# First six projection units side by side, and a 64-row matmul inside both MLPs of a two-layer trunk

## The chip, the cores and the metric

The kernel runs on one core of a Trainium2 chip. The metric is the device time of one execution in microseconds (us). The kernel before has a median of 2397.32 us over 3 runs (2397.16 to 2398.94).

## The reference, cut to what matters

Two decoder layers run on one sequence of 256 tokens with model width 2048, all in float32:

```
for layer in range(2):
    h = rms_norm(x, norm_mix[layer])
    if layer == 0:
        u = h @ w_in_a                       # one projection for both head groups
        y = concat(nsa(u_nsa), rwkv7(u_rw)) @ w_out_a
    else:
        u = h @ w_in_b
        y = concat(rglru(u_lru), hgrn2(u_hg)) @ w_out_b
    x = x + y
    h2 = rms_norm(x, norm_mlp[layer])
    z = relu(h2 @ w_ff1[layer])              # 2048 -> 8192
    x = x + (z * z) @ w_ff2[layer]           # 8192 -> 2048
```

`rwkv7` mixes each token with the one before it, sends a part of its columns through small low-rank matrices (96, 96 and 256 wide) and runs a recurrence over 16 heads of 64. `nsa` is attention over compressed, selected and windowed keys. Nearly all of the arithmetic lies in the dense projections and in the MLPs.

## The kernel before, in words

Activations are kept transposed: 2048 features are 16 blocks ("k") of 128 partitions, with the 256 tokens along the free axis. A dense product is cut into **units** of 128 output columns. One unit reads 1 MB of weights in two halves; `load` (L123) issues one DMA per half on SyncE's queue into a pool of four buffers.

**Three products for one.** The array takes a rounded float32 format, so each operand is split into a high and a low part. `split` (L128) makes `wh` with a ScalarE copy (L130) and `wl` with a VectorE subtraction (L132), each into a pool of two buffers. An operand tile holds the activations' high part in its columns 0 to 255 and the low part in columns 256 to 511. `mm3` (L147) then runs for each k one pass of `wh` over 512 columns (L152) and one pass of `wl` over 256 columns (L153), both into one PSUM bank. Such a pass pair is called a pair here; a unit has 16 pairs. `evac` (L163) folds the bank into one 256-column tile with a ScalarE copy (L167) and a VectorE add (L168).

**The norm is late.** `prepare` (L192) scales x by the gain alone and splits it (L193 on ScalarE, L194 on VectorE). The mean square goes through a matmul with a matrix of ones (`rstd_of`, L206), and the factor 1/rms is multiplied in when a unit is evacuated (L306). So units can run before the norm is known.

**The start.** x comes in eight DMAs of 2 blocks (L255). The first unit's halves lie between them in the queue, then the second unit's, then the constants (L259). All sixteen blocks are prepared, with one split among each eight; unit 0 runs, the squares (L263 to L269) and unit 1's splits follow, then unit 1, the norm's matmul, units 2 and 3 and, in `rwkv_a` (L310), the rest. The first four units are the low-rank columns; from unit 4 on, three units (r, k, v) belong to each of eight steps j. Each j has low-rank matmuls of 96 rows (L350, L354), a chain of gates on ScalarE and VectorE, and a group under `behind()` (L378), which gets a lower priority and ends in 64-row matmuls (L425) and in DMAs to DRAM on GpSimd's queue. The recurrence's small systems are then solved on VectorE (`rw_solve`, L437) while TensorE goes on with the attention's units; `rwkv_b` (L450) needs the solution, fetched back at L466.

**The MLP.** `mlp` (L934) runs four blocks of 16 up-units and 16 down-units, 2048 pairs per layer, as one unbroken stream; the norm's matmul (L206) of the MLP lies among the first unit's pairs.

**The order.** The framework's planner orders each engine's instructions when the kernel is built, by priority (program order, moved by `high_priority` and `behind`) and by its own estimate of when operands are ready. Each engine then runs its own list strictly in that order. PSUM has eight banks: two with the tag "mm" for units and two each with "ga", "gb" and "gc". `keep_in_program_order` pins an instruction behind the one written before it on the same engine; `issue_after` queues what a block issues on an engine behind a given instruction, as an order alone.

Of the kernel before, what the change touches and what calls it, by code (L numbers as in the profile page):

```python
# [10 lines left out]
F32 = mybir.dt.float32  # L11
F32R = mybir.dt.float32r
# [7 lines left out]
P = 128  # L20
T = 256
D = 2048
KT = D // P
# [29 lines left out]
CON, NCON = _cols(_CON)  # L53
HG_LEVELS = (1, 2, 4, 8, 16, 32)
RWP_N = 4 * 512 + 4


@with_exitstack
def kernel(
# [52 lines left out]
    def bank(name, tag="ga"):  # L112
        return pg.tile([P, 512], F32, tag=tag, name=name)
# [6 lines left out]
        return [t[:, k] for t in (half_of(pool, f"{name}_{h}") for h in range(2)) for k in range(8)]  # L120


    def load(src, h, name, pool=None):  # L123
        raw = (pool or wraw).tile([P, 8, P], F32, tag="raw", name=f"raw_{name}_{h}")
        nc.sync.dma_start(raw, src[:, h * 1024 : (h + 1) * 1024].rearrange("p (b c) -> p b c", c=P))
        return raw

    def split(raw, h, name):  # L128
# [23 lines left out]
            M.matmul(ps, wh, mv, start=first, stop=False)  # L152
        M.matmul(ps[:, :T], wl, mv[:, :T], start=False, stop=last)  # L153

    def unit(src, mv, name, folded=False, tag=None, parts=None, pool=None):
        ps = bank(f"mm_{name}", tag) if tag else pmm.tile([P, 512], F32, tag="mm", name=f"mm_{name}")
        parts = parts or stream(src, name, pool)
        for k in range(KT):
            wh, wl = parts[k // 8]
            mm3(ps, wh[:, k % 8], wl[:, k % 8], mv[k], k == 0, k == KT - 1, folded)  # L160
        return ps

# [38 lines left out]
        A.activation(sq, x, AF.Square)  # L201
        V.tensor_add(acc, acc, sq)

    def rstd_of(acc, name):
        ps = bank(f"ms_{name}")
        M.matmul(ps[:, :T], ones, acc, start=True, stop=True)  # L206
        v = ev.tile([P, T], F32, tag="t", name=f"v_{name}")
        V.tensor_scalar(v, ps[:, :T], 1.0 / D, EPS, op0=ALU.mult, op1=ALU.add)
        r0 = ev.tile([P, T], F32, tag="s", name=f"r0_{name}")
        rsqrt_of(r0, v, 1.0, zero_b, name, ev)  # L210
        q = ev.tile([P, T], F32, tag="sq", name=f"q_{name}")
        V.tensor_mul(q, r0, r0)
        V.scalar_tensor_tensor(q, q, -0.5, v, ALU.mult, ALU.mult)
        r = ev.tile([P, T], F32, tag="rstd", name=f"rstd_{name}")
        V.scalar_tensor_tensor(r, q, 1.5, r0, ALU.add, ALU.mult)
        return r
# [15 lines left out]
    def layer0_mix():  # L232
        with ExitStack() as st:
            mx = st.enter_context(tc.tile_pool(name="mx", bufs=1))
            acc, hx = norm("a0")
            rwp_d = [dram.tile([P, 2, RWP_N], F32, name=f"rwp_d{j}") for j in range(4)]
            pm_d = [dram.tile([P, 2, 8, P], F32, name=f"pm_d{j}") for j in range(4)]
            z_d = dram.tile([P, 32, 32], F32, name="z_d")

            gate = mx.tile([P, T], F32, name="gate", bufs=1)  # L240
            nb = mx.tile([P, 32, 32], F32, name="nb", bufs=1)
            yr = half_of(big, "yr")
            cw = big.tile([P, 4, 8, P], F32, tag="half", name="cw")

            def load_cw(w):
                nc.sync.dma_start(cw.rearrange("p b l e -> p b (l e)"), cmp_w[w].rearrange("b p n -> p b n"))

            with tc.tile_pool(name="pa", bufs=1) as pa:
                xi = [pa.tile([P, 8, T], F32, tag="rwp", name=f"xi_{i}", bufs=2) for i in range(2)]
                raws = []  # L250
                first = []
                with tc.high_priority(10**6):
                    for i in range(2):
                        for b in range(4):
                            nc.sync.dma_start(xi[i][:, 2 * b : 2 * b + 2], xT[:, 8 * i + 2 * b : 8 * i + 2 * b + 2])  # L255
                        raws.append(load(w_in0[0], i, "i0_0"))
                    for i in range(2):
                        raws.append(load(w_in0[1], i, "i0_1"))
                    nc.sync.dma_start(con, consts)  # L259

                    def squares(i):
                        sq = pa.tile([P, 4, T], F32, tag="pm", name=f"sq_a0_{i}", bufs=2)
                        A.activation(sq, xi[i // 2][:, 4 * (i % 2) : 4 * (i % 2) + 4], AF.Square)  # L263
                        V.tensor_add(sq[:, 0:2], sq[:, 0:2], sq[:, 2:4])
                        if i == 0:
                            V.tensor_add(acc, sq[:, 0], sq[:, 1])
                        else:
                            V.tensor_add(sq[:, 0], sq[:, 0], sq[:, 1])
                            V.tensor_add(acc, acc, sq[:, 0])  # L269

                    parts = []
                    for i in range(2):
                        for j in range(8):
                            prepare(hx, 8 * i + j, xi[i][:, j], "gmix0")
                            if j == 3:
                                parts.append(split(raws[i], i, "i0_0"))
                    first.append(unit(None, hx, "i0_0", parts=parts))
                    squares(0)
                    parts = [split(raws[2], 0, "i0_1")]
                    squares(1)  # L280
                    parts.append(split(raws[3], 1, "i0_1"))
                    first.append(unit(None, hx, "i0_1", parts=parts))
                    squares(2)
                    squares(3)
                    rstd = rstd_of(acc, "a0")
                first.append(unit(w_in0[2], hx, "i0_2", tag="ga"))
                first.append(unit(w_in0[3], hx, "i0_3", tag="gb"))
                rwkv_a(pa, gate, hx, scaled_by(rstd), rwp_d, pm_d, nb, first, load_cw)
            with tc.tile_pool(name="pb", bufs=1) as pb, tc.tile_pool(name="pn", bufs=1) as pn:
                rw_solve(pb, nb, z_d)  # L290
                for j in range(0, 8, 2):
                    rwkv_b(pb, j, rwp_d, pm_d, z_d, yr)
                kv = nsa_keys(pn, mx, hx, scaled_by(rstd), gate, cw, load_cw)
                yn = half_of(big, "yn")
                for j in range(8):
                    nsa_head(pn, mx, hx, scaled_by(rstd), kv, j, yn)
        return [t[:, k] for t in (yn, yr) for k in range(8)]
# [9 lines left out]

        return scaled

    def rwkv_a(pa, gate, hx, scaled, rwp_d, pm_d, nb, first, load_cw):  # L310
        def tl(tag, shape=(P, T), bufs=1, name=None):
            return pa.tile(list(shape), F32, tag=tag, name=name or tag, bufs=bufs)

        def shifted(u, name, mu, out, rows=P):
            ub = tl("ub", (P, T + 1), 3, name=f"ub_{name}")
            G.memset(ub[:, 0:1], 0.0)
            scaled(first[u] if u < 4 else unit(w_in0[u], hx, f"i0_{u}"), ub[:, 1:], name)
            d = tl("d", bufs=2, name=f"d_{name}")
            V.tensor_sub(d[:rows], ub[:rows, 0:T], ub[:rows, 1:])
            V.scalar_tensor_tensor(out[:rows], d[:rows], p_("mu", mu)[:rows], ub[:rows, 1:], ALU.mult, ALU.add)  # L320
            return ub
# [15 lines left out]
        for j in range(8):  # L337
# [5 lines left out]
            pm = tl("pm", (P, 8, P), 2, name=f"pm_{j}")  # L343
            js = slice(j * P, (j + 1) * P)
            w2j = tl("w2j", (P, P), 2, name=f"w2_{j}")
            nc.scalar.dma_start(w2j[:96], rw_w2[:, js])
            a2j = tl("a2j", (P, P), 2, name=f"a2_{j}")
            nc.scalar.dma_start(a2j[:96], rw_a2[:, js])
            ps = bk_(f"lora_{j}")
            M.matmul(ps[:, :T], w2j[:96], th[:96], start=True, stop=True)  # L350
            sg = tl("sg", bufs=2, name=f"sg_{j}")
# [26 lines left out]
            with behind():  # L378
# [28 lines left out]
                nc.scalar.dma_start(g2j, rw_g2[:, :, j * P : (j + 1) * P])  # L407
# [526 lines left out]
    def mlp(layer, xs, hx, rstd, nxt, zp, zraw):  # L934
        z = {}

        def up(q):
            zq = z[q] = operand(big if q % 2 == 0 else zp, f"z_{layer}_{q}")
            for k in range(KT):
                n = f"f1_{layer}_{q}_{k}"  # L940
                s = evac(unit(w_ff1[layer, q * KT + k], hx, n, pool=zraw), n)
                V.tensor_mul(s, s, rstd)  # L942
                V.scalar_tensor_tensor(s, s, 0.0, s, ALU.max, ALU.mult)
                split_to(zq[k], s)

# [12 lines left out]
        down(1)  # L958
        up(3)
        down(2)  # L960
        down(3)
# [45 lines left out]
def _layout(i):  # L1007
# [17 lines left out]
    out["w_in0"] = _chunks(np.concatenate(cols, axis=1))  # L1025
# [108 lines left out]
```

## Time and profile before

| what | value |
|---|---|
| median of 3 runs | 2397.32 us |
| the profiled execution, its own time | 2415.31 us |
| its span, first to last instruction | 2413.5 us |
| TensorE busy | 2390.6 us (99%) |
| VectorE busy | 1697.7 us (70%) |
| ScalarE busy | 1243.7 us (52%) |
| mean granted TensorE clock | 0.997 |

The span is the time between the first and the last instruction of the profiled execution. Its own time is 1.8 us longer. Busy shares are means over stages with different limits. The end of a matmul in the trace is modelled and reaches into the next one, so the distance from start to start is what tells how fast a stream of passes runs.

### The profile page before, as it was taken

The numbers are of one execution on the slowest core, as the hardware profiler recorded it, in microseconds if no ns is written. First come the engines' busy times: TensorE is split into PE (matmuls) and PEld (weight loads), VectorE is DVE, ScalarE is ACT, GpSimd is POOL, SyncE is SP. The second block draws the span as 40 slices with busy tenths as digits, with TensorE's granted clock in tenths as the row PEclk, the third lists the DMA queues.
The fourth block names the chain that finished last, engine by engine and source line by source line (L and its number), as shares of the span: only waits on it lengthen the run. The fifth ranks groups of instructions, "written<-read, shape, count | busy, mean of one in ns | idle before, by whom it ended". The sixth has DMA issues, their size and how long they took to land.

```text
span 2413.5 us, 37947 instructions
## 1 busy us (share of the span) xinstructions
PE 2390.6 (99%) x14386; PEld 2072.1 (86%) x14386; DVE 1697.7 (70%) x3006; ACT 1243.7 (52%) x2152; POOL 44.9 (2%) x118
## 2 busy tenths in 40 slices
PE   8999999999999999999999999999999999999999
PEld 6888877798888888888888888889888888888888
DVE  7887865677676576576568888788777667667555
ACT  7554455555444444444456666675544444444443
POOL 0112010000000000000000000000000000000000
PEclk9999999999999999999999999999999999999999
DMA  7667743465555555655555444456556555656564
GB/s 263 212 216 228 246 139 105 155 209 183 190 184 186 188 184 187 188 185 187 187 176 187 150 151 153 154 168 217 185 191 191 189 188 191 192 187 190 191 199 134
DMA packets 125862, 446.77 MB, mean 185 GB/s; under 512 B 14192, under 2 KB 19952, under 8 KB 124016
## 3 DMA queue, kind: packets, MB, share of 16 engines
q1 hardware_dynamic: 115824, 414.06, 53.7%
q0 software_dynamic: 5456, 26.79, 3.1%
q10 hardware_dynamic: 4400, 3.50, 0.4%
q8 instruction: 114, 1.87, 0.3%
q14 instruction: 68, 0.56, 0.1%
HBM read 429.06 MB, written 15.22 MB: 184 GB/s over the span
## 4 chain that ended last, share of the span: by engine, by line
PE 93%; DVE 3%; DMA 2%; ACT 1%; issue 1%; POOL 0%; DVEq 0%; ACTq 0%; POOLq 0%
PE mm_f L152 39%; PE mm_f L153 20%; PE mm_i L152 13%; PE mm_i L153 7%; PE mm_o L153 2%; PE mm_o L152 1%; PE mm_o L149 1%; PE mm_o L150 1%; DVE wl_i L132 1%; PE hl L816 1%; PE pair L425 1%; DMA rwp<-rwp_d 1%; PE psx L496 0%; ACT wh_o L130 0%; PE psu L503 0%
## 5 line engine op out<-in xcount | busy, mean ns | idle before, releaser
L132 DVE TENSOR_TENSOR wl_f<-raw_f,wh_f 128x1024 fp32r<-128x1024 f32 x512 | 627.2, 1225 | 486.1 <-ACT wh_f L130 486.1
L130 ACT CAST wh_f<-raw_f 128x1024 fp32r<-128x1024 f32 x512 | 538.6, 1052 | 773.4 <-PE mm_f L152 566.8
L152 PE MATMUL mm_f<-hx_m,wh_f 128*128 128x512 f32 x2048 | 717.2, 395 | 0.0
L152 PE MATMUL mm_f<-z,wh_f 128*128 128x512 f32 x2048 | 717.1, 395 | 0.0
L152 PE MATMUL mm_i<-hx_a,wh_i 128*128 128x512 f32 x1536 | 563.9, 405 | 11.5 <-ACT wh_i L130 11.4
L153 PE MATMUL mm_f<-hx_m,wl_f 128*128 128x256 f32 x2048 | 574.8, 281 | 0.0
L153 PE MATMUL mm_f<-z,wl_f 128*128 128x256 f32 x2048 | 574.4, 280 | 0.0
L152 PEld LDWEIGHTS mm_f<-z,wh_f 128*128 128x128 f32 x2048 | 383.9, 187 | 90.0
L152 PEld LDWEIGHTS mm_f<-hx_m,wh_f 128*128 128x128 f32 x2048 | 383.9, 187 | 90.0
L153 PE MATMUL mm_i<-hx_a,wl_i 128*128 128x256 f32 x1536 | 447.6, 291 | 1.2 <-DVE wl_i L132 1.0
L153 PEld LDWEIGHTS mm_f<-hx_m,wl_f 128*128 128x128 f32 x2048 | 387.0, 189 | 0.1
L153 PEld LDWEIGHTS mm_f<-z,wl_f 128*128 128x128 f32 x2048 | 387.0, 189 | 0.0
L152 PEld LDWEIGHTS mm_i<-hx_a,wh_i 128*128 128x128 f32 x1536 | 289.8, 189 | 72.3 <-ACT wh_i L130 12.1
L153 PEld LDWEIGHTS mm_i<-hx_a,wl_i 128*128 128x128 f32 x1536 | 291.5, 190 | 9.3 <-DVE wl_i L132 4.0
L130 ACT CAST wh_i<-raw_i 128x1024 fp32r<-128x1024 f32 x192 | 201.3, 1049 | 188.9 <-PE mm_i L152 169.5
L132 DVE TENSOR_TENSOR wl_i<-raw_i,wh_i 128x1024 fp32r<-128x1024 f32 x192 | 234.5, 1222 | 80.6 <-ACT wh_i L130 76.4
L168 DVE TENSOR_TENSOR s_f<-mm_f,t_f 128x256 f32<-128x256 f32 x256 | 106.7, 417 | 3.0 <-ACT t_f L167 3.0
L132 DVE TENSOR_TENSOR wl_o<-raw_o,wh_o 128x1024 fp32r<-128x1024 f32 x64 | 78.3, 1223 | 32.6 <-ACT wh_o L130 32.3
L130 ACT CAST wh_o<-raw_o 128x1024 fp32r<-128x1024 f32 x64 | 67.2, 1050 | 63.3 <-issue 29.2
L167 ACT COPY t_f<-mm_f 128x256 f32<-128x256 f32 x256 | 93.2, 364 | 4.3 <-PE mm_f L153 4.3
L153 PE MATMUL mm_o<-ym,wl_o 128*128 128x256 f32 x256 | 72.6, 284 | 0.8 <-DVE wl_o L132 0.8
L942 DVE TENSOR_TENSOR s_f<-s_f,rstd_m 128x256 f32<-128x256 f32 x128 | 54.4, 425 | 4.4
(420 smaller groups left out, 2254.7 us busy)
## 6 DMA issues: line engine op xcount, KB each, us to landing
raw_f<-in_w_ff_dram SPq DMA_DIRECT2D x512, 512.0 KB, 4.5
raw_i<-in_w_in_dram SPq DMA_DIRECT2D x192, 512.0 KB, 4.1
raw_o<-in_w_out_dram SPq DMA_DIRECT2D x64, 512.0 KB, 4.2
rwp_d<-rwp POOLq DMA_DIRECT2D x8, 1026.0 KB, 7.1
rwp<-rwp_d POOLq DMA_DIRECT2D x4, 1540.0 KB, 10.7
cw<-in_cmp_w_dram SPq DMA_DIRECT2D x2, 2048.0 KB, 10.2
pm_d<-pm POOLq DMA_DIRECT2D x8, 512.0 KB, 6.3
pm<-pm_d POOLq DMA_DIRECT2D x4, 1024.0 KB, 5.3
```

The source lines that it names most:

```text
L130: A.copy(wh, raw)
L132: V.tensor_sub(wl, raw, wh)
L149: M.matmul(ps[:, :T], wh, mv[:, :T], start=first, stop=False)
L150: M.matmul(ps[:, :T], wh, mv[:, T:], start=False, stop=False)
L152: M.matmul(ps, wh, mv, start=first, stop=False)
L153: M.matmul(ps[:, :T], wl, mv[:, :T], start=False, stop=last)
L167: A.copy(t, ps[:, T:])
L168: V.tensor_add(s, ps[:, :T], t)
L425: M.matmul(pps[q][:, c * P : (c + 1) * P], bk[hs, c], ar[hs, c], start=True, stop=True)
L816: M.matmul(pl[:, x * T + i * P : x * T + (i + 1) * P], qk[:, ii], qk[:, ii], start=True, stop=True)
L942: V.tensor_mul(s, s, rstd)
```

## The change

**The first six units** run side by side. Their weights are laid out in DRAM so that block k of all six is one contiguous piece of 128 x 768 (a layout of the inputs, made before the launch). Sixteen DMAs bring them, one for each k, with the DMA of x's two blocks ahead of each even k and the constants behind k = 9. For each k the block is prepared, 768 columns are split at once, and six pairs go into six PSUM banks. Ahead of it, sixteen 128 x 128 matmuls of a zeroed tile are issued. The norm's matmul takes a bank of tag "gc", and a seventh unit follows it ahead of `rwkv_a`.

**DMAs.** The small low-rank weights on ScalarE's queue are issued behind the first copy of the start (`anchor`). The compression weights `cw` are issued behind the last weight load written before them.

**Both MLPs** get one matmul of 64 rows and 128 columns, between the `wh` and the `wl` pass of k = 4 in the second unit of the first block.

```diff
+NFIRST = 6
+    last_load = [None]
-        nc.sync.dma_start(raw, src[:, h * 1024 : ...])
+        last_load[0] = nc.sync.dma_start(raw, src[:, h * 1024 : ...])
+    def narrow(name):
+        ps = bank(f"nar_{name}")
+        tc.keep_in_program_order(M.matmul(ps[:, 0:P], ident[0:64], ident[0:64], start=True, stop=True))
     def unit(...):
+            if k == part_at:
+                M.matmul(ps, wh[:, k % 8], mv[k], start=False, stop=False)
+                narrow(name)
+                tc.keep_in_program_order(M.matmul(ps[:, :T], wl[:, k % 8], mv[k][:, :T], start=False, stop=False))
+                continue
     def load_cw(w):
+        with tc.issue_after(last_load[0].ins):
             nc.sync.dma_start(cw..., cmp_w[w]...)
+    wrm = pa.tile([P, P], F32, name="wrm")
+    V.memset(wrm, 0.0)
     with tc.high_priority(10**6):
-        for i in range(2):                       # x and the first unit's halves, then the second unit's
-            ...
-        nc.sync.dma_start(con, consts)
+        for k in range(KT):
+            if k % 2 == 0:
+                nc.sync.dma_start(xi[k // 8][:, k % 8 : k % 8 + 2], xT[:, k : k + 2])
+            nc.sync.dma_start(raw[:, :NFIRST], w_k[k].rearrange("p (b c) -> p b c", c=P))
+            if k == 9:
+                nc.sync.dma_start(con, consts)
+        for i in range(16):
+            M.matmul(pw[:, :P], wrm, wrm, start=True, stop=True)
-        ...                                      # sixteen prepares with two splits, unit 0, squares, unit 1
+        for k in range(KT):
+            prepare(hx, k, xi[k // 8][:, k % 8], "gmix0")
+            ins = A.copy(wh[:, :NFIRST], raws[k][:, :NFIRST])
+            anchor = anchor or ins.ins
+            V.tensor_sub(wl[:, :NFIRST], raws[k][:, :NFIRST], wh[:, :NFIRST])
+            for u in range(NFIRST):
+                mm3(first[u], wh[:, u], wl[:, u], hx[k], k == 0, k == KT - 1)
+            if k % 4 == 3:
+                squares(k // 4)
-        rstd = rstd_of(acc, "a0")
-    first.append(unit(w_in0[2], hx, "i0_2", tag="ga"))
-    first.append(unit(w_in0[3], hx, "i0_3", tag="gb"))
+        rstd = rstd_of(acc, "a0", "gc")
+    first.append(unit(w_in0[NFIRST], hx, f"i0_{NFIRST}", tag="gb"))
     ...
-        nc.scalar.dma_start(w2j[:96], rw_w2[:, js])
+        with tc.issue_after(anchor):             # the same for a2j and g2j
+            nc.scalar.dma_start(w2j[:96], rw_w2[:, js])
     ...
-        s = evac(unit(w_ff1[layer, q * KT + k], hx, n, pool=zraw), n)
+        s = evac(unit(w_ff1[layer, q * KT + k], hx, n, pool=zraw, part_at=4 if q == 0 and k == 1 else None), n)
```

## Rows read from the trace of the kernel before

**Rows 1.** Windows by stage: length, busy us (x instructions) per engine, PEclk, DMA share, GB/s.
```profile
4.00:40.00 36.00, 27.94 (x141) 23.08 (x142) 30.07 (x58) 26.38 (x42) 0.44 (x3) 1.00 0.90 322
40.00:73.00 33.00, 33.00 (x188) 28.59 (x188) 27.57 (x46) 21.57 (x42) 0.74 (x6) 1.00 0.63 192
73.00:227.00 154.00, 153.45 (x891) 130.96 (x890) 124.49 (x238) 84.27 (x166) 19.59 (x49) 1.00 0.67 215
```
**Rows 2.** Windows, instructions of L152 alone, within each MLP: length, PE, PEld busy.
```profile
570.00:1270.00 700.00, 700.00 (x1983) 372.30 (x1982) 1.00 0.59 186
1705.00:2405.00 700.00, 700.00 (x2020) 377.58 (x2020) 1.00 0.59 188
```
**Rows 3.** Timeline, PE, at the two MLPs' norm matmul: start, us, what.
```profile
562.25 0.70 PE L206 MATMUL ms_m<-acc_m,con 128*128 128x256 f32 x2
562.60 0.47 PE L153 MATMUL mm_f<-hx_m,wl_f 128*128 128x256 f32 x1
...
1701.51 0.70 PE L206 MATMUL ms_m<-acc_m,con 128*128 128x256 f32 x2
```
**Rows 4.** Timeline, PE, 64-row matmuls between wh and wl, and 34 pairs on.
```profile
81.84 0.39 PE L152 MATMUL mm_i<-hx_a,wh_i 128*128 128x512 f32 x1
82.16 1.16 PE L425 MATMUL pair<-rwp,bk 64*128 64x128 f32 x8
83.25 0.39 PE L153 MATMUL mm_i<-hx_a,wl_i 128*128 128x256 f32 x1
83.47 0.39 PE L152 MATMUL mm_i<-hx_a,wh_i 128*128 128x512 f32 x1
...
95.26 0.39 PE L152 MATMUL mm_i<-hx_a,wh_i 128*128 128x512 f32 x1
```
**Rows 5.** Timeline, PE, 64-row matmuls between wl and wh, and three pairs.
```profile
174.64 1.16 PE L425 MATMUL pair<-rwp,bk 64*128 64x128 f32 x8
175.72 0.50 PE L152 MATMUL mm_i<-hx_a,wh_i 128*128 128x512 f32 x1
...
176.18 0.40 PE L152 MATMUL mm_i<-hx_a,wh_i 128*128 128x512 f32 x1
...
177.24 0.40 PE L152 MATMUL mm_i<-hx_a,wh_i 128*128 128x512 f32 x1
```
**Rows 6.** Timeline, PE, from unit 0's first pass to unit 6's last.
```profile
10.92 0.80 PE L152 MATMUL mm_i<-hx_a,wh_i 128*128 128x512 f32 x1 [10.92 <-ACT wh_i L130]
...
17.36 0.49 PE L152 MATMUL mm_i<-hx_a,wh_i 128*128 128x512 f32 x1 [0.44 <-ACT wh_i L130]
...
56.06 0.28 PE L153 MATMUL mm_i<-hx_a,wl_i 128*128 128x256 f32 x1
```
**Rows 7.** Timeline, PE, pairs in unit 0, and a low-rank matmul.
```profile
14.48 0.63 PE L152 MATMUL mm_i<-hx_a,wh_i 128*128 128x512 f32 x1
15.09 0.39 PE L152 MATMUL mm_i<-hx_a,wh_i 128*128 128x512 f32 x1
15.44 0.40 PE L152 MATMUL mm_i<-hx_a,wh_i 128*128 128x512 f32 x1
...
47.46 0.60 PE L350 MATMUL lora<-th,w 96*128 96x256 f32 x2
47.97 0.39 PE L153 MATMUL mm_i<-hx_a,wl_i 128*128 128x256 f32 x1
```
**Rows 8.** Windows of the first 6 us, columns as in rows 1.
```profile
0.00:3.00 3.00, 0.00 (x0) 0.00 (x0) 0.00 (x0) 1.28 (x1) 0.70 (x14) 1.00 0.35 58
3.00:6.00 3.00, 0.00 (x0) 0.00 (x0) 0.00 (x0) 0.00 (x0) 0.00 (x0) 1.00 0.98 341
```
**Rows 9.** Groups between 10 and 60 us: busy, mean ns, idle before.
```profile
L132 DVE TENSOR_TENSOR wl_i<-raw_i,wh_i 128x1024 fp32r<-128x1024 f32 x16 | 19.5, 1221 | 3.2 <-ACT wh_i L130 2.7
L130 ACT CAST wh_i<-raw_i 128x1024 fp32r<-128x1024 f32 x17 | 17.7, 1049 | 8.3 <-PE mm_i L152 7.3 <-DMA raw_i<-in_w_in_dram 0.9
```
**Rows 10.** Waits of PE between 227 and 318 us: total, times, longest.
```profile
PE psh L478 <- DVE zat L467: 1.1, 1, 1.1
```

More of the change, by code (lines that the diff above doesn't have):

```diff
@@ L120, in operand @@
         return [t[:, k] for t in (half_of(pool, f"{name}_{h}") for h in range(2)) for k in range(8)]
+    last_load = [None]
     def load(src, h, name, pool=None):
         raw = (pool or wraw).tile([P, 8, P], F32, tag="raw", name=f"raw_{name}_{h}")
-        nc.sync.dma_start(raw, src[:, h * 1024 : (h + 1) * 1024].rearrange("p (b c) -> p b c", c=P))
+        last_load[0] = nc.sync.dma_start(raw, src[:, h * 1024 : (h + 1) * 1024].rearrange("p (b c) -> p b c", c=P))
         return raw
@@ L153, in mm3, with unit @@
         M.matmul(ps[:, :T], wl, mv[:, :T], start=False, stop=last)
-    def unit(src, mv, name, folded=False, tag=None, parts=None, pool=None):
+    def narrow(name):
+        ps = bank(f"nar_{name}")
+        tc.keep_in_program_order(M.matmul(ps[:, 0:P], ident[0:64], ident[0:64], start=True, stop=True))
+    def unit(src, mv, name, folded=False, tag=None, parts=None, pool=None, part_at=None):
         ps = bank(f"mm_{name}", tag) if tag else pmm.tile([P, 512], F32, tag="mm", name=f"mm_{name}")
@@ L202, in square_sum, with rstd_of @@
         V.tensor_add(acc, acc, sq)
-    def rstd_of(acc, name):
-        ps = bank(f"ms_{name}")
+    def rstd_of(acc, name, tag="ga"):
+        ps = bank(f"ms_{name}", tag)
         M.matmul(ps[:, :T], ones, acc, start=True, stop=True)
@@ L245, in load_cw @@
             def load_cw(w):
-                nc.sync.dma_start(cw.rearrange("p b l e -> p b (l e)"), cmp_w[w].rearrange("b p n -> p b n"))
+                with tc.issue_after(last_load[0].ins):
+                    nc.sync.dma_start(cw.rearrange("p b l e -> p b (l e)"), cmp_w[w].rearrange("b p n -> p b n"))
             with tc.tile_pool(name="pa", bufs=1) as pa:
                 xi = [pa.tile([P, 8, T], F32, tag="rwp", name=f"xi_{i}", bufs=2) for i in range(2)]
+                w_k = w_in0[0:NFIRST].rearrange("n p m -> (n p m)").rearrange("(k p c) -> k p c", k=KT, p=P)
+                first = [
+                    pmm.tile([P, 512], F32, tag="mm", name=f"mm_i0_{u}") if u < 2 else bank(f"mm_i0_{u}", ("ga", "gb", "gc")[(u - 2) % 3])
+                    for u in range(NFIRST)
+                ]
+                wrm = pa.tile([P, P], F32, name="wrm")
+                V.memset(wrm, 0.0)
+                pw = bank("warm", "gc")
                 raws = []
-                first = []
+                anchor = None
                 with tc.high_priority(10**6):
-                    for i in range(2):
[L254 to L258, printed above, removed]
-                    nc.sync.dma_start(con, consts)
+                    for k in range(KT):
+                        if k % 2 == 0:
+                            nc.sync.dma_start(xi[k // 8][:, k % 8 : k % 8 + 2], xT[:, k : k + 2])
+                        raw = wraw.tile([P, 8, P], F32, tag="raw", name=f"raw_i0_f{k}")
+                        nc.sync.dma_start(raw[:, :NFIRST], w_k[k].rearrange("p (b c) -> p b c", c=P))
+                        raws.append(raw)
+                        if k == 9:
+                            nc.sync.dma_start(con, consts)
+                    for i in range(16):
+                        M.matmul(pw[:, :P], wrm, wrm, start=True, stop=True)
                     def squares(i):
@@ L269, in squares @@
                             V.tensor_add(acc, acc, sq[:, 0])
[L271 to L284, printed above, removed]
-                    rstd = rstd_of(acc, "a0")
-                first.append(unit(w_in0[2], hx, "i0_2", tag="ga"))
-                first.append(unit(w_in0[3], hx, "i0_3", tag="gb"))
-                rwkv_a(pa, gate, hx, scaled_by(rstd), rwp_d, pm_d, nb, first, load_cw)
+                    for k in range(KT):
+                        prepare(hx, k, xi[k // 8][:, k % 8], "gmix0")
+                        wh = wspl.tile([P, 8, P], F32R, tag="wh", name=f"wh_i0_f{k}")
+                        ins = A.copy(wh[:, :NFIRST], raws[k][:, :NFIRST])
+                        anchor = anchor or ins.ins
+                        wl = wspl.tile([P, 8, P], F32R, tag="wl", name=f"wl_i0_f{k}")
+                        V.tensor_sub(wl[:, :NFIRST], raws[k][:, :NFIRST], wh[:, :NFIRST])
[5 more added lines that the diff above has]
+                first.append(unit(w_in0[NFIRST], hx, f"i0_{NFIRST}", tag="gb"))
+                rwkv_a(pa, gate, hx, scaled_by(rstd), rwp_d, pm_d, nb, first, load_cw, anchor)
             with tc.tile_pool(name="pb", bufs=1) as pb, tc.tile_pool(name="pn", bufs=1) as pn:
@@ L308, in scaled_by, with rwkv_a @@
         return scaled
-    def rwkv_a(pa, gate, hx, scaled, rwp_d, pm_d, nb, first, load_cw):
+    def rwkv_a(pa, gate, hx, scaled, rwp_d, pm_d, nb, first, load_cw, anchor):
         def tl(tag, shape=(P, T), bufs=1, name=None):
@@ L316, in shifted @@
             G.memset(ub[:, 0:1], 0.0)
-            scaled(first[u] if u < 4 else unit(w_in0[u], hx, f"i0_{u}"), ub[:, 1:], name)
+            scaled(first[u] if u < len(first) else unit(w_in0[u], hx, f"i0_{u}"), ub[:, 1:], name)
             d = tl("d", bufs=2, name=f"d_{name}")
@@ L345, in rwkv_a @@
             w2j = tl("w2j", (P, P), 2, name=f"w2_{j}")
-            nc.scalar.dma_start(w2j[:96], rw_w2[:, js])
             a2j = tl("a2j", (P, P), 2, name=f"a2_{j}")
-            nc.scalar.dma_start(a2j[:96], rw_a2[:, js])
+            with tc.issue_after(anchor):
+                nc.scalar.dma_start(w2j[:96], rw_w2[:, js])
+                nc.scalar.dma_start(a2j[:96], rw_a2[:, js])
             ps = bk_(f"lora_{j}")
@@ L406, in rwkv_a @@
                 g2j = tl("g2j", (P, 2, P), 2, name=f"g2_{j}")
-                nc.scalar.dma_start(g2j, rw_g2[:, :, j * P : (j + 1) * P])
+                with tc.issue_after(anchor):
+                    nc.scalar.dma_start(g2j, rw_g2[:, :, j * P : (j + 1) * P])
                 psg = bk_(f"gg_{j}")
@@ L1024, in _layout @@
     cols.append(nsa[:, :1024])
-    out["w_in0"] = _chunks(np.concatenate(cols, axis=1))
+    cols = np.concatenate(cols, axis=1)
+    w_in0 = _chunks(cols)
+    w_in0[:NFIRST] = cols[:, : NFIRST * P].reshape(NFIRST, P, D)
+    out["w_in0"] = w_in0
     w = a["w_in_b"][0]
```

## The prediction

> **What bounds the kernel now.** I read the page's shares first, then windows by stage, then TensorE's timeline. TensorE (PE) is busy for 99% of the span, but a busy PE says little about speed, so I counted passes. From 40 to 227 us PE is without a gap (33.00 of 33.00 and 153.45 of 154.00 us) while VectorE is at 84% and then 81% [rows 1]. So a microsecond taken from PE's list before 227 us moves all that follows, as long as VectorE can follow. There are two places in which PE loses time.
>
> The first is the start. PE's first pass begins at 10.92 us, unit 1 at 17.36 us, and unit 6's last pass at 56.06 us [rows 6]. The seven units to there are 112 pairs.
>
> The second is the cadence of the same stream of pairs. In 700 us of layer 0's MLP 1983 `wh` passes run, in 700 us of layer 1's 2020 [rows 2]: 0.3530 against 0.3465 us a pair, with PE full, the granted clock 1.00 and the same code. Each cadence holds for a whole MLP. Where it changes, another matmul stood in the stream, and for matmuls with fewer than 128 rows the trace shows a rule. Where 64-row matmuls stand between a pair's `wh` and its `wl`, the stream leaves them fast: 34 pairs from 83.47 to 95.26 us are 0.3468 each [rows 4]; eight such places are in the trace (two with 32 rows or in another loop), and all eight leave the fast cadence. Where they stand between `wl` and the next `wh`, it leaves slow: 1.06 us for three pairs, 0.353 each [rows 5], three places of three. Matmuls of 128 rows leave either: the norm's matmul stands at 562.25 us with `wl` next, ahead of the slow MLP, and in the same way at 1701.51 us ahead of the fast one [rows 3].
>
> **The change part by part.** *The start, before.* 112 pairs at 0.3465 are 38.8 us. The norm's matmul and three low-rank ones lie among them; one such two-pass matmul takes 0.51 us from its start to the next pass [rows 7], so four take 2.0. 56.06 + 0.23 for the last pass - 38.8 - 2.0 = 15.5 us lost.
>
> *The start, after.* The first block needs two blocks of x (262 KB), the parameters (152 KB) and 393 KB of weights: 807 KB. The first 3 us move 174 KB, then 341 KB each us [rows 8], so it is there at 3 + 633/341 = 4.9, with some 0.4 to land 5.3 us. The copy and the subtraction of 1024 columns take 1.05 and 1.22 us [rows 9]; for 768 I scale to 0.79 and 0.92. So `wh` is ready at 6.1, `wl` at 7.0 us, and from there PE is the slowest: a block is 6 x 0.3465 = 2.08 us of PE, 0.524 MB or 1.5 us of DMA, and on ScalarE and VectorE one such split, one operation of 256 columns and a share of the squares (256 columns more for each k): by columns from the same rows 1.3 and 1.5 us, still 0.5 below PE. Before the first `wl` one `wh` pass of 0.23 is done, so 6.8 us are lost. The norm's matmul costs as before. The seventh unit's split starts when the buffer of k = 14 is free and has one block (2.08 us) for 1.05 + 1.22 us: 0.2 us late.
>
> The sixteen zero matmuls are 32 passes. None is in the trace. From above they cost 2 us more than the data's wait if they don't raise the clock; from below they gain 2. Unit 0 shows what is at stake: a pair takes 0.61 us up to 15.09 and 0.35 after it [rows 7], some four us after PE's first pass, though the clock's column says 1.00 from the first window on; I read the earlier pairs as the lower of TensorE's two levels. At about 0.11 us a pass (0.14 with the switch, eight in 1.09 us [rows 4]) and twice that at the lower level, 32 passes from about 1 us on end between 5 and 8.5 us, around the 6.1 at which data arrive. I take 0.4 us late. Lost after: 6.8 + 0.2 + 0.4 = 7.4. The start is worth 15.5 - 7.4 = 8.1 us.
>
> *What is late next.* Up to 40 us VectorE has done 30.07 us of work and to 73 us another 27.57 [rows 1], about where PE reaches the first 64-row matmuls. After the change it has the same splits and products in the start (some 25 us of work by 40.5 us), and all of the seven evacuations and the norm's chain behind them. Without a gap it would be where it was at 73 us at 40.5 + (57.6 - 25) = 73 again, not 8 us earlier. PE need not wait for that: it has units 7 to 11, 28 us, to run, and the banks of tag "mm" come free early since an evacuation has priority. Later VectorE has 19% to spare over 154 us, 29 us. So the loss is 0 if units fill the gap and 8.1 if they don't; the nearest row is PE without a gap while VectorE is at 84%, so I take 1.0.
>
> *DMAs.* The low-rank loads leave ScalarE's way at the start: its first activation is bound by data then. They cost three DMA issues in ScalarE's list later, beside a PE-bound stream: nothing. `cw`'s first load (2 MB) moves out of the start, behind unit 15's weights in SyncE's queue; it is needed only by the attention's units, behind 227 us: nothing. Its second load holds the weight loads queued behind it for as long as its buffer is in use, as before. If that cover went, it would cost a landing, under 1 us.
>
> *The 64-row matmuls.* Two passes between `wh` and `wl`. Eight passes at 82.16 us: from `wh` at 81.84 to the next `wh` at 83.47 is 1.63 us instead of 0.35 [rows 4], so 1.28 extra; six passes fewer at 0.11 to 0.14 leave 0.5 to 0.6. Two MLPs: 1.2 us. The Trainium skill (TensorE: Matmul & The Clock Gate, "What overlaps and what doesn't") says that a weight load overlaps a running matmul only when the row groups differ, or goes to the background buffer; by its first half the 64-row load, whose rows lie within the 128, would wait, and the trace agrees, 0.32 us from `wh` to the first 64-row pass. It makes the sum no other.
>
> *What they give.* 2048 - 21 = 2027 pairs come behind the matmul in layer 0's MLP; 0.3530 - 0.3465 = 0.0065 us each is 13.2 us, if that MLP would be slow. In layer 1's it gives nothing where that is fast.
>
> **The sum, and the profiled execution against the runs.** For the profiled execution: 2415.3 - 8.1 + 1.0 + 1.2 - 13.2 = 2396.2 us. But its own time of 2415.3 is 18.0 above the median of the runs. Either profiling costs 18 us evenly, or the runs had layer 0's MLP fast: 13.2 of the 18.0 is just that, and the cadence is set by something that may fall otherwise without a profiler. I hold the second likelier, since PE's passes in a full stream are the last thing that a profile would stretch by 0.75%, and since three runs lie within 1.8 us of each other. The Trainium skill (Runtime: NRT & Kernel Launch, "The ~15µs preamble/postamble breakdown") has a gap of about 6.2 us between a profile's total and the reported time, whatever the kernel; by it 11.8 of the 18.0 would be left to explain, nearer to one MLP's cadence than to none. No run here shows such a gap by itself.
>
> So for the runs: 2397.3 - 8.1 + 1.0 + 1.2 = 2391.4 us.
>
> **The rivals.**
> *The runs were slow in one MLP too.* Then the matmul takes another 13.2 us: 2378.2. For it: the profiled execution is slow there. Against it: the 18.0 us.
> *The lead of the start is lost to VectorE.* At the first 64-row matmuls PE has to wait in its fixed order, or the solver's chain does: PE waits 1.1 us for it at its end already [rows 10]. The price is the whole 8.1: 2397.3 + 1.2 = 2398.5. Against it: units 7 to 11, and the 19%.
> *The 64-row matmul leaves the slow cadence behind where it was fast.* All eight fast places have eight passes or more ahead of the return to 128 rows; two passes are a single matmul, and two-pass matmuls of 128 rows leave either cadence. Place: each MLP's second unit; price 13.2 for each MLP that turns; it decides from one MLP on, since 13.2 is more than the 5.9 gained: 2391.4 + 13.2 = 2404.6, slower than before. Against it: the switch of rows back to 128 and the place between `wh` and `wl` are the same.
> *The zero matmuls don't raise the clock*: 2 us less, 2393.4, within the forecast's own range.
>
> **How the numbers follow.** The forecast has 0.47, its own range 2388 to 2396 (loss to VectorE 0 to 4, clock -1 to 2). The slow MLP in the runs has 0.30 (2374 to 2383), the lost lead 0.13, the slow cadence 0.10. About 0.2%, 4.8 us, is what a measurement can tell, so faster means under 2392.5: 0.68 of the forecast, all of the second case: 0.62. Same: the rest of the forecast and most of the lost lead: 0.26. Slower, over 2402.1: 0.12. The range runs from 2374 to 2398.
>
> **What would show it.** Right: the zero matmuls from about 1 us, the first real pass by 7 us, the seventh unit's last pass near 47 us with the norm's matmul alone ahead of it; about 2020 `wh` passes in 700 us of both MLPs; a two-pass 64-row matmul with some 0.5 us around it; no PE gap over 1 us before 227 us; the solver's chain still ending near PE's wait. Wrong: 1983 passes in either MLP behind the matmul (the rule fails), pairs at 0.6 us behind the zero matmuls, or the first low-rank or 64-row matmuls with PE idle ahead of them. A run under 2385 us would say that the runs before were slow in an MLP too.

## The result, and the profile after

The changed kernel takes **2423.12 us** (median of 4 runs, 2421.45 to 2423.32) where the kernel before took 2397.24 us beside it (4 runs, 2396.81 to 2398.94): a ratio of 1.0105, 95% interval 1.0088 to 1.0123. It is 25.9 us slower. The forecast was 2391 us and its range ended at 2398. The profiled execution is one of the four runs: 2423.32 us, span 2421.3 us, granted clock 1.00.

In the new kernel the lines have moved: `mm3` is L155 (`wh`) and L156 (`wl`), the norm's matmul L219, the new 64-row matmul L161 between L169 (`wh`) and L171 (`wl`), the front's split L300 and L303. The windows by stage, to be held against [rows 1], then the first 6 us against [rows 8], have the columns of rows 1:

```profile
4.00:40.00 36.00, 34.12 (x192) 28.70 (x192) 25.83 (x42) 23.03 (x36) 0.00 (x0) 1.00 0.87 288
40.00:73.00 33.00, 32.46 (x182) 28.00 (x181) 30.36 (x61) 26.38 (x53) 1.04 (x7) 1.00 0.58 183
73.00:227.00 154.00, 150.76 (x875) 127.79 (x874) 125.50 (x243) 84.62 (x167) 19.90 (x51) 1.00 0.71 228
0.00:3.00 3.00, 1.94 (x9) 1.95 (x10) 0.17 (x1) 1.28 (x1) 0.70 (x14) 1.00 0.30 58
3.00:6.00 3.00, 3.00 (x20) 3.00 (x20) 0.48 (x1) 0.90 (x2) 0.00 (x0) 1.00 0.99 373
```

PE is busy from the start (34.12 of 36 us instead of 27.94), but it has gaps where it had none: 0.54 us between 40 and 73 us and 3.24 us from there to 227. VectorE is at 92% between 40 and 73 us, where it was at 84%.

The loss is in the MLPs. These are the passes of L155 alone in 700 us of each MLP, the answer to [rows 2]:

```profile
570.00:1270.00 700.00, 700.00 (x1983) 372.29 (x1982) 1.00 0.58 185
1705.00:2405.00 700.00, 700.00 (x1982) 372.30 (x1982) 1.00 0.58 186
```

Before, one MLP had 1983 and the other 2020. Now both have the low count, at a granted clock of 1.00, so the clock is not the cause. PE's timeline at the first MLP's norm matmul and the new matmul shows where the stream turns (start, us, engine, line; the answer to [rows 3]):

```profile
555.75 0.70 PE L219 MATMUL ms_m<-acc_m,con 128*128 128x256 f32 x2
...
556.40 0.40 PE L155 MATMUL mm_f<-hx_m,wh_f 128*128 128x512 f32 x1
...
559.87 0.39 PE L155 MATMUL mm_f<-hx_m,wh_f 128*128 128x512 f32 x1
...
560.22 0.39 PE L169 MATMUL mm_f<-hx_m,wh_f 128*128 128x512 f32 x1
560.54 0.48 PE L161 MATMUL nar_f<-con 64*128 64x128 f32 x2
560.95 0.39 PE L171 MATMUL mm_f<-hx_m,wl_f 128*128 128x256 f32 x1
```

From 556.40 to 559.87 lie ten pairs, 0.347 us each: behind the norm's matmul the stream is fast. Behind the 64-row matmul it takes 0.3533 us a pair up to the MLP's end. The second MLP does the same: 0.347 up to 1699.86, the 64-row matmul at 1700.18, 0.3533 from there on. From the first to the last pair an MLP now takes 353.94 ns a pair (the matmul included) where the fast one before takes 347.05: 6.89 ns x 2047 = 14.1 us, and 28.2 us for both. The start gives back 1.5 us in this trace (the last matmul of the j steps' groups stands at 225.61 us instead of 227.07) and 3.0 in e1_no_narrow's (below), so the sum is +25.2 to +26.7; measured are +25.9.

### The profile page after: what moved, and what is told of

Read it like the earlier page. It is cut to its first block, busy times and chain, and to the rows that moved or that the text cites. A ratio compares the mean times of both kernels' runs of the same rounds, so it can differ in the third digit from the quotient of the medians.

```text
span 2421.3 us, 38037 instructions
## 1 busy us (share of the span) xinstructions
PE 2405.3 (99%) x14422; PEld 2074.8 (86%) x14422; DVE 1697.1 (70%) x3011; ACT 1244.5 (51%) x2156; POOL 45.1 (2%) x118
## 4 chain that ended last, share of the span: by engine, by line
PE 91%; DVE 4%; DMA 2%; ACT 2%; issue 1%; POOL 0%; ACTq 0%; SPq 0%; DVEq 0%; POOLq 0%
PE mm_f L155 40%; PE mm_f L156 20%; PE mm_i L155 11%; PE mm_i L156 6%; PE mm_o L156 2%; PE mm_o L155 2%; PE mm_o L152 1%; PE mm_o L153 1%; DVE wl_i L135 1%; DMA rwp_d<-rwp 1%; PE hl L840 1%; DMA rwp<-rwp_d 1%; DMA xi<-in_xT_dram 1%; PE psx L520 0%; PE pair L449 0%
## 5 line engine op out<-in xcount | busy, mean ns | idle before, releaser
L155 PE MATMUL mm_f<-z,wh_f 128*128 128x512 f32 x2048 | 723.9, 399 | 0.0
L155 PE MATMUL mm_f<-hx_m,wh_f 128*128 128x512 f32 x2046 | 723.2, 399 | 0.0
L156 PE MATMUL mm_f<-z,wl_f 128*128 128x256 f32 x2048 | 575.2, 281 | 0.0
L156 PE MATMUL mm_f<-hx_m,wl_f 128*128 128x256 f32 x2046 | 575.0, 281 | 0.0
L155 PE MATMUL mm_i<-hx_a,wh_i 128*128 128x512 f32 x1440 | 528.2, 404 | 0.9 <-ACT wh_i L133 0.8
L155 PEld LDWEIGHTS mm_f<-z,wh_f 128*128 128x128 f32 x2048 | 384.8, 188 | 96.0
L155 PEld LDWEIGHTS mm_f<-hx_m,wh_f 128*128 128x128 f32 x2046 | 384.5, 188 | 95.7
L156 PE MATMUL mm_i<-hx_a,wl_i 128*128 128x256 f32 x1440 | 419.6, 291 | 1.1 <-DVE wl_i L135 1.0
L156 PEld LDWEIGHTS mm_f<-z,wl_f 128*128 128x128 f32 x2048 | 386.9, 189 | 0.0
L156 PEld LDWEIGHTS mm_f<-hx_m,wl_f 128*128 128x128 f32 x2046 | 386.5, 189 | 0.1
L155 PEld LDWEIGHTS mm_i<-hx_a,wh_i 128*128 128x128 f32 x1440 | 270.7, 188 | 58.2 <-issue 1.1
L156 PEld LDWEIGHTS mm_i<-hx_a,wl_i 128*128 128x128 f32 x1440 | 272.5, 189 | 8.0 <-DVE wl_i L135 3.3
L133 ACT CAST wh_i<-raw_i 128x1024 fp32r<-128x1024 f32 x180 | 188.9, 1049 | 173.3 <-PE mm_i L155 151.8
L135 DVE TENSOR_TENSOR wl_i<-raw_i,wh_i 128x1024 fp32r<-128x1024 f32 x180 | 220.0, 1222 | 73.3 <-ACT wh_i L133 68.8
L156 PE MATMUL mm_o<-ym,wl_o 128*128 128x256 f32 x256 | 72.7, 284 | 0.9 <-DVE wl_o L135 0.9
L967 DVE SCALAR_TENSOR_TENSOR s_f<-s_f 128x256 f32<-128x256 f32 x128 | 54.4, 425 | 4.4
```

Of the source, the lines that this page charges most:

```text
L133: A.copy(wh, raw)
L135: V.tensor_sub(wl, raw, wh)
```

## The experiments

Runs of the kernel before spread: 17 of all 73 lie above 2409 us, the others mostly at 2396 to 2399, and its two profiles show the first MLP once at the slow and once at the fast cadence. So each result stands with its runs.

**e1_no_narrow**: after without its 64-row matmul.

```diff
-s = evac(unit(w_ff1[layer, q * KT + k], hx, n, pool=zraw, part_at=4 if q == 0 and k == 1 else None), n)
+s = evac(unit(w_ff1[layer, q * KT + k], hx, n, pool=zraw), n)
```

> The changed kernel without the 64-row matmul in the MLPs. Theory A (the matmul itself leaves the slow cadence behind): both MLPs fast, 0.3465 us a pair, and about 2395 us, that is 2397.2 less the 1.5 us by which the last 64-row group before the solver comes earlier in the changed kernel's trace. Rival B (the slow cadence comes from the changed start, which shifts when the norm's matmul falls; the 64-row matmul does nothing): both MLPs stay at 0.353 and the time stays near 2422. Theory C on the start (the whole lead of 6.6 us at unit 6 reaches the end, and the other 5 us are lost elsewhere): 2390.5.

Measured: 2396.62 us (12 runs), ratio 0.9985 (0.996 to 1.0009). Eight runs lie at 2392.5 to 2397.2 (median 2394.4), four at 2406.2 to 2408.5. L155 in its MLPs:

```profile
570.00:1270.00 700.00, 699.80 (x2020) 377.43 (x2019) 1.00 0.59 188
1683.00:2383.00 700.00, 700.00 (x2021) 377.63 (x2020) 1.00 0.59 188
```

Both are fast. Against the eight, after is 28.7 us slower: the 64-row matmul accounts for all of the loss.

**e2_narrow_alone**: before with the 64-row matmul in both MLPs and nothing else (the `narrow` and `part_at` lines of the change).

> The kernel before with the 64-row matmul in both MLPs and nothing else. Theory A: both MLPs at 0.353 us a pair behind the matmul, two times 2027 x 0.0065 = 26.4 us and 1.2 us for the two matmuls themselves: about 2425 us. Rival B: 2398.5 us, or 2397.2 less 13 if an MLP was slow in the runs.

Measured: 2426.46 us (4 runs, 2425.75 to 2431.23), ratio 1.0107 (1.0069 to 1.0146). Its MLPs (L152 is its `wh`):

```profile
570.00:1270.00 700.00, 700.00 (x1983) 372.29 (x1982) 1.00 0.58 185
1710.00:2410.00 700.00, 700.00 (x1982) 372.25 (x1982) 1.00 0.58 186
```

The same loss without the new start.

**e3_before_again**: the kernel before, one more profile.

> The kernel before once more, for a second trace of it. If the 18 us between its profiled execution and its runs are the cadence of layer 0's MLP and the stretch of 10 us at half clock, a profiled execution at about 2397 us shows both MLPs at 0.3465 us a pair and a clock of 1.00 throughout. If they are a price of profiling, this one is near 2415 us too.

Measured: 2402.5 us, span 2400.7 us, granted clock 0.998; both MLPs at 347.04 and 347.05 ns a pair. So a profiled execution can have both MLPs fast. The first profile's excess of 18.0 us is one MLP's cadence, about 13.6 us (6.63 ns a pair), and some 5 us of this stretch at half the clock, found in the first trace:

```profile
318.80:329.10 10.30, 10.30 (x72) 7.43 (x71) 4.19 (x27) 3.87 (x18) 0.00 (x0) 0.50 0.17 52
```

The second profile has such a stretch too, from 318.6 to 328.8 us; it stands for the 5 us by which this execution lies above the runs' 2397.

**e4_probe**: before, with one of eleven kinds of probe (one of them: none), shuffled, at the fifth pair of each of the MLPs' 256 units.

```diff
+    def probe(name, n, rows):
+        ps = bank(f"nar_{name}")
+        for i in range(n):
+            tc.keep_in_program_order(M.matmul(ps[:, i * P : (i + 1) * P], ident[0:rows], ident[0:rows], start=True, stop=True))
     def unit(...):
+            if at and k == 4:      # probe, then wh, wl ("before"); or wh, probe, wl ("between")
+                ...
```

> The kernel before with a probe at the fifth pair of nearly every unit of both MLPs (256 units, eleven kinds in a shuffled order: none; 1, 2, 3 or 4 matmuls of 64 rows between wh and wl; 1 or 4 of them ahead of wh; 1 of 128 rows between, 1 ahead; 1 of 32 rows between; 4 of 128 rows between). What is computed stays the reference. Theory A: one of 64 rows between wh and wl leaves 0.353 whatever the cadence was before, four of them (eight passes, as in the 64-row groups of the trace of before) leave 0.3465, and none leaves the cadence as it was. Rival B: the cadence behind a kind is either one with about even chances, for all kinds.

Measured: 2590.87 us, one execution. Units without a probe kept their cadence. For each probe, the pairs' mean distance in the stretch ahead of it and behind it, F about 346.7 and S about 353.3 ns:

```
matmuls x rows           S>F  F>S  F>F  S>S
between  1 x 64            9   10    3    1   turns
between  2 x 64            1    0   10   12   keeps
between  3 x 64           11   11    0    2   turns
between  4 x 64            4    0   15    4   keeps fast, slow in half
between  1 x 32            1    0   17    5   keeps
between  1 x 128          11    9    2    0   turns
between  4 x 128          11    0   12    0   leaves fast
before   1 x 64            0   16    0    8   leaves slow
before   4 x 64           13    9    0    0   turns
before   1 x 128           4   11    1    8   mostly slow
```

One of the ten that turn from fast to slow, `wh` passes and probe alone:

```profile
840.12 0.39 PE L157 MATMUL mm_f<-z,wh_f 128*128 128x512 f32 x1
...
842.20 0.39 PE L175 MATMUL mm_f<-z,wh_f 128*128 128x512 f32 x1
842.52 0.49 PE L164 MATMUL nar_f<-con 64*128 64x128 f32 x2
843.16 0.39 PE L157 MATMUL mm_f<-z,wh_f 128*128 128x512 f32 x1
...
845.28 0.40 PE L157 MATMUL mm_f<-z,wh_f 128*128 128x512 f32 x1
```

Six pairs in 2.08 us, 0.347 each, ahead of it; six in 2.12, 0.353 each, behind it. So it is neither the rows nor the place alone: one 64-row matmul between the passes mostly turns the cadence over, two mostly keep it, three mostly turn it, and four of 128 rows leave it fast whatever it was.

The single distances say more than the means. The slow stream comes in a beat of three, about 350, 361 and 349 ns; the fast one is even, 346 to 347 ns, or goes 343 and 350 in turn. Here are the six most telling kinds between the passes, by the stream ahead of the probe (in the slow one, by the number of distances since the last one of 361 ns), with the cadence behind it and how often:

```
matmuls x rows   even      343/350   slow: 0   slow: 1   slow: 2
1 x 64           slow 10   fast 3    fast 2    fast 7    slow 1
2 x 64           fast 8    fast 2    -         slow 12   fast 1
3 x 64           slow 11   -         fast 2    fast 9    slow 2
4 x 64           fast 13   fast 2    fast 3    slow 4    fast 1
1 x 128          slow 9    fast 2    -         fast 11   -
4 x 128          fast 12   -         fast 3    fast 7    fast 1
```

No field has two outcomes, nor has one of the other four kinds. So the exceptions to "turns" and "keeps" are not chance: what a probe leaves goes with where it falls in the stream.

**g1_two_narrow**: after with two 64-row matmuls in place of the one. It puts "turns over" against "slows down" at the place of the change.

```diff
-        tc.keep_in_program_order(M.matmul(ps[:, 0:P], ident[0:64], ident[0:64], start=True, stop=True))
+        for i in range(2):
+            tc.keep_in_program_order(M.matmul(ps[:, i * P : (i + 1) * P], ident[0:64], ident[0:64], start=True, stop=True))
```

> After with two 64-row matmuls in a row in place of the one, in both MLPs. Theory (the cadence of the pairs is turned over by one such matmul, and two turn it over and back): both MLPs stay at the cadence that they had ahead of the place, fast in most executions, so 347.0 to 347.3 ns a pair and 2395 to 2397 us, with single runs some 12 us higher as in e1_no_narrow. Rival (any 64-row matmul at this place leaves the slow cadence): two do no better than one, 2423 to 2425 us, 353.9 ns a pair in both MLPs.

Measured: 2395.19 us (10 runs, 2394.32 to 2396.73). More of the same matmul takes 27.9 us off after's time. Its MLPs:

```profile
570.00:1270.00 700.00, 699.80 (x2019) 377.35 (x2019) 1.00 0.58 189
1683.00:2383.00 700.00, 698.86 (x2017) 376.96 (x2016) 1.00 0.58 188
```

The ratio to before is 0.9946 (0.9921 to 0.9971), but ten of before's 19 runs beside it were above 2409 us; against its other nine (median 2398.3) the gain is 3.1 us, 0.13%.

Its first MLP fits neither theory as it was stated. The norm's matmul left the stream slow there, and the two matmuls did not keep it so:

```profile
555.65 0.40 PE L155 MATMUL mm_f<-hx_m,wh_f 128*128 128x512 f32 x1
...
557.77 0.40 PE L170 MATMUL mm_f<-hx_m,wh_f 128*128 128x512 f32 x1
558.10 0.71 PE L162 MATMUL nar_f<-con 64*128 64x128 f32 x4
...
560.35 0.39 PE L155 MATMUL mm_f<-hx_m,wh_f 128*128 128x512 f32 x1
...
562.43 0.39 PE L155 MATMUL mm_f<-hx_m,wh_f 128*128 128x512 f32 x1
```

Six pairs take 2.12 us ahead of them and 2.08 behind. The place lies two distances after the long one, where e4_probe's two matmuls also left the fast cadence.

**g2_narrow_mlp0**: after with its 64-row matmul in the first MLP alone.

```diff
-part_at=4 if q == 0 and k == 1 else None
+part_at=4 if q == 0 and k == 1 and layer == 0 else None
```

> After with its 64-row matmul in the first MLP alone. Theory: the first MLP runs at 353.9 ns a pair and the second at 347.1, so one of the two steps of some 14 us is left: 2408 to 2411 us. Rival (the cadence is carried from the first MLP through the output pass into the second): both slow, 2422 to 2424 us.

Measured: 2408.31 us (10 runs, 2406.78 to 2410.06), half of the loss. In its trace (L155) the first MLP is slow, and the second, without the matmul, is fast:

```profile
570.00:1270.00 700.00, 700.00 (x1982) 372.28 (x1982) 1.00 0.58 184
1699.00:2399.00 700.00, 700.00 (x2020) 377.55 (x2019) 1.00 0.59 188
```

But the first MLP was slow ahead of the matmul already, and it did not turn it:

```profile
557.85 0.40 PE L155 MATMUL mm_f<-hx_m,wh_f 128*128 128x512 f32 x1
...
559.97 0.40 PE L169 MATMUL mm_f<-hx_m,wh_f 128*128 128x512 f32 x1
560.30 0.48 PE L161 MATMUL nar_f<-con 64*128 64x128 f32 x2
...
560.94 0.39 PE L155 MATMUL mm_f<-hx_m,wh_f 128*128 128x512 f32 x1
...
563.06 0.40 PE L155 MATMUL mm_f<-hx_m,wh_f 128*128 128x512 f32 x1
```

Six pairs take 2.12 us on either side, again two distances after the long one. So at this place one 64-row matmul leaves the slow cadence whichever it meets (fast in both MLPs of after and of e2_narrow_alone, slow here), and two leave the fast one. That fits the runs, which a plain turn would not: every run of after, e2_narrow_alone and g2_narrow_mlp0 has the loss, and all ten of g1_two_narrow are without it, though before and e1_no_narrow have a part of their runs slow.

**f1_setter**: after with four matmuls of 128 rows in place of the 64-row one. **f2_setter_before**: the same four in the kernel before.

```diff
-        tc.keep_in_program_order(M.matmul(ps[:, 0:P], ident[0:64], ident[0:64], start=True, stop=True))
+        for i in range(4):
+            tc.keep_in_program_order(M.matmul(ps[:, i * P : (i + 1) * P], ident, ident, start=True, stop=True))
```

> The changed kernel with four matmuls of 128 rows and 128 columns in place of the one of 64 rows, at the same place in both MLPs. Theory A2 (from the probe: eight passes of 128 rows between wh and wl leave the fast cadence 23 times of 23, whatever it was before): both MLPs at 0.3465 us a pair in every run; the runs of the changed kernel without any such matmul at 2392.5 to 2397.2 us, plus 0.8 us for each of two such groups, so 2394 to 2399 us, and none near 2407 us. Rival B2 (the probe's place within a stream that is probed every 16 pairs matters): still some runs 14 us higher.

> The kernel before with the same four matmuls in both MLPs and nothing else. Theory A2: 2398 to 2401 us and no run at 2411 to 2417, as some runs of before are. The difference to the changed kernel with the same matmuls is the start alone: 3.0 us by the traces (the last 64-row group of the recurrence at 224.0 instead of 227.1 us).

Measured: 2395.53 us (11 runs), ratio 0.9996 (0.9978 to 1.0013), and 2399.82 us (11 runs, 2397.08 to 2403.92), ratio 1.0012 (1.0003 to 1.0021). Both MLPs are at 347.5 ns a pair in both, matmuls included. One run of f1 stands at 2414.11, at a granted clock of 0.991; no other of the 22 lies above 2404. The four matmuls cost 0.89 us an MLP (1.24 us from `wh` to the next `wh` instead of 0.35). In the kernel before they bring no gain by the median, since most of its runs were fast without them. The two kernels differ by the start alone: 4.3 us by the medians, where 3.0 were expected.

**f3_x_ahead**: f1 with the last six DMAs of x ahead of the fifth weight load.

```diff
-                        if k % 2 == 0:
-                            nc.sync.dma_start(xi[k // 8][:, k % 8 : k % 8 + 2], xT[:, k : k + 2])
+                        for kx in {0: (0,), 2: (2,), 4: (4, 6, 8, 10, 12, 14)}.get(k, ()):
+                            nc.sync.dma_start(xi[kx // 8][:, kx % 8 : kx % 8 + 2], xT[:, kx : kx + 2])
```

> The changed kernel with the four matmuls, and x's last six DMAs issued ahead of the fifth weight load. Theory D (x's DMAs stand in SyncE's queue behind weight loads that wait for a buffer, so ScalarE waits for x and the split's low part is late): ScalarE's waits for x of 1.1 to 1.3 us go, the six units end 1 to 2 us earlier than 42.9 us, and some of it, 0 to 1.5 us, reaches the end, since a later wait takes part of it (the buffer that goes to DRAM, waited for 2.0 us at 111 us). Rival E (the splits wait for PE to free their two buffers): the six units end where they did and nothing changes.

Measured: 2394.99 us (11 runs, 2393.29 to 2397.92), ratio 0.9985 (0.9973 to 0.9997). The first six units end at 43.50 us, not earlier than f1's 42.82: ScalarE's waits for x fall from 3.0 to 1.0 us, but those for the weights behind them rise from 0.3 to 1.6. A miss as an edit of the start.

**f4_no_zero**: f1 without its sixteen zero matmuls.

```diff
-                    for i in range(16):
-                        M.matmul(pw[:, :P], wrm, wrm, start=True, stop=True)
```

> The changed kernel with the four matmuls in the MLPs and without the sixteen zero matmuls of the start. If they raise the clock: the first pairs take 0.6 us for about 4 us, the six units end 1 to 2 us later, and the time is 0 to 2 us more. If they only delay the data's first pass: up to 1 us earlier.

Measured: 2395.35 us (11 runs, 2393.2 to 2397.93), ratio 0.999 (0.9981 to 0.9999). PE's first passes in it:

```profile
6.24 1.22 PE L155 MATMUL mm_i<-hx_a,wh_i_f 128*128 128x512 f32 x2 [6.24 <-ACT wh_i_f L298]
...
7.83 0.63 PE L155 MATMUL mm_i<-hx_a,wh_i_f 128*128 128x512 f32 x1
8.47 0.63 PE L155 MATMUL mm_i<-hx_a,wh_i_f 128*128 128x512 f32 x1
```

Pairs take 0.64 us up to 11.67, in the changed kernel 0.35 from 7.83 on (next section). Yet the six units end at 43.52 us, hardly later than with the zero matmuls (42.82 in f1's trace, 43.44 in the changed kernel's own), and the whole runs do not differ. The 1 to 2 us that were expected are not there.

## Why the prediction was wrong

**The step that failed** is the cadence rule: "Where 64-row matmuls stand between a pair's `wh` and its `wl`, the stream leaves them fast ...; eight such places are in the trace ..., and all eight leave the fast cadence." I read the cadence behind the eight places and not ahead of them. Ahead of those in the j steps it was fast as well: from 48.19 to 174.64 us before's pairs come at 0.347 wherever nothing stands among them, ahead of the place of [rows 4] too. Those places are groups of eight passes and more; four 64-row matmuls keep a fast cadence in 15 of 15 cases of e4_probe. The change inserts one matmul, two passes, and one makes an even fast stream slow: 10 of 10 times in e4_probe (the three fast cases that stayed fast had the 343/350 form), and in both MLPs of after and of e2_narrow_alone. The rival that named this, that "two passes are a single matmul", was priced at 13.2 us an MLP and given 0.10. Measured are 13.5 us (2027 pairs at 6.66 ns) and 0.6 us for the matmul itself, and it took both MLPs, since in each of them the norm's matmul had made the stream fast; g2_narrow_mlp0 shows that a slow one would have stayed slow. In the sum the two matmuls stood with 1.2 us; they cost 28.2.

**Why the norm's matmul looked as if it set nothing.** In [rows 3] it stands ahead of a slow and of a fast MLP. Behind the layer's output projection both MLPs begin slow (354 ns a pair in before, after and e1_no_narrow); in the first MLP the norm's two passes turn it fast in after and e1_no_narrow and left it slow in before's first profile, in g1_two_narrow's and in g2_narrow_mlp0's. That is a single two-pass matmul of the kind that turns the cadence or not by where it falls. It is the likely reason why executions of before fall at about 2397 or about 2412 us; what decides in one execution stays open.

**The 18.0 us** were read rightly: they were no even price of profiling, and the runs had that MLP fast as a rule. They are one MLP's cadence and the half-clock stretch. The Trainium skill (Runtime: NRT & Kernel Launch, "The ~15µs preamble/postamble breakdown") has a gap of about 6.2 us between a profile's total and the reported time. That is between two readings of one execution; the 18.0 us lie between the own times of different executions, so the gap has no part in them. No run here shows it: own time less span is 1.7 to 2.1 us in each of the twelve profiled executions.

**The start** was right in its mechanism and too large in size: 8.1 us forecast, 5.7 there at unit 6 and 3.0 left at 227 us in one trace; by the runs of f1_setter and f2_setter_before it is worth 4.3. In e1_no_narrow, whose start is the change's, unit 6's last pass stands at 48.84 us instead of 56.06 [rows 6]; 1.5 of these 7.2 us are three low-rank matmuls, 0.51 each [rows 7], that now come later. The last matmul of the j steps' groups stands at 224.03 us instead of 227.07 (223.09 to 225.61 in the seven traces with the new start, f3's and f4's among them; 226.42 to 227.51 in the four of the old one without probes). PE in the changed kernel itself, as [rows 6, 7]:

```profile
1.06 5.73 PE L285 MATMUL warm<-wrm 128*128 128x128 f32 x32 [1.06 <-DVE wrm L271]
6.54 0.71 PE L155 MATMUL mm_i<-hx_a,wh_i_f 128*128 128x512 f32 x2
7.49 0.50 PE L156 MATMUL mm_i<-hx_a,wl_i_f 128*128 128x256 f32 x2 [0.23 <-DVE wl_i_f L303]
7.83 0.39 PE L155 MATMUL mm_i<-hx_a,wh_i_f 128*128 128x512 f32 x1
8.17 0.39 PE L155 MATMUL mm_i<-hx_a,wh_i_f 128*128 128x512 f32 x1
```

The zero matmuls do raise the clock, as the pairs of 0.64 us without them show, and the first pass comes within the 7 us that I gave it. The 0.4 us for the data to land stand in no row; the first copy of weights began at 5.61 us where the sum had 5.3. What I had not priced is the order of SyncE's queue, here in e1_no_narrow:

```profile
3.69 0.48 SPq L278 DMA_DIRECT2D xi<-in_xT_dram  x1
7.43 1.59 SPq L280 DMA_DIRECT2D raw_i_f<-in_w_in_dram  x2
9.08 0.42 SPq L278 DMA_DIRECT2D xi<-in_xT_dram  x1
11.77 1.77 SPq L280 DMA_DIRECT2D raw_i_f<-in_w_in_dram  x2
13.98 0.33 SPq L278 DMA_DIRECT2D xi<-in_xT_dram  x1
```

A weight load that waits for a buffer holds x behind it (the queue's waits on the subtraction L303 come to 13.0 us), the split then comes late, and PE waits: at six places of e1_no_narrow's front two `wh` passes stand 0.3 to 0.8 us further apart than 0.347, together 2.9 us. f3_x_ahead shows that moving x alone only moves the wait to the weights.

**The loss to VectorE** was taken as 1.0 us, with both ends 0 and 8.1; it is 2.7 us (5.7 less 3.0) in e1_no_narrow's trace. PE's waits up to 230 us in e1_no_narrow, with the line waited for, total, count and longest:

```profile
PE ptv L440 <- ACT rwp L435: 1.3, 1, 1.3
...
PE mm_i L156 <- DVE wl_i L135: 0.8, 1, 0.8
...
PE lora L373 <- ACT th L352: 0.4, 1, 0.4
```

and VectorE's between 73 and 120 us:

```profile
DVE rwp L402 <- DMA rwp_d<-rwp: 3.5, 2, 2.0
```

VectorE has time in the mean (82% busy), but it stands in order behind the write of a buffer to DRAM, the next split stands behind that, and PE, which came early, waits. The cadence has little part in it: between unit 6 and the last group the slower pairs add 0.8 us in e1_no_narrow and 0.6 in before. No run takes these waits away, so this part is read from the trace and not tested. The wait for the solver [rows 10] has fallen from 1.1 to 0.3 us in after, so that was not the place. The 3.0 us last to the end: e1's eight lower runs have 2394.4 us against the 2397.3 that the forecast went by.

**The 64-row matmuls' own cost**, 0.5 to 0.6 us forecast, is 0.6: `wh` at 560.22 to `wl` at 560.95 is 0.73 us instead of 0.23, and from there the next `wh` takes 0.22 instead of 0.12.

## What to carry to other kernels

Before you take a rule on cause from places in a trace, read the state ahead of each place too: a place that keeps a state and one that makes it look the same behind. Read single distances as well as means, since two streams of the same mean came out differently here. Count what you insert in the unit in which the examples came (here single matmuls, not "64-row matmuls"). And a lead at the start is worth what is left of it at the next place where an engine in strict order waits for something that did not get earlier.

## What the runs showed of the hardware that was not expected

A stream of one 512-column and one 256-column pass has two stable cadences at the same granted clock of 1.00, 346.7 and 353.3 ns a pair, 1.9% apart, and holds either over 2000 pairs. A single two-pass matmul between the two passes turns one into the other (19 of 23 with 64 rows, 20 of 22 with 128), two keep it (22 of 23), and four of 128 rows leave the fast one (23 of 23, and of the 44 runs of the four kernels with them one is above 2404 us). The exceptions go with the place in the stream: the slow one has a beat of three pairs, the fast one two forms, and in all 231 probes between or ahead of the passes the same kind at the same place left the same cadence. What in the engine keeps the cadence no run here shows.
